# A batched matmul with transposed operands: both casts first, and the copies out of PSUM on two engines

## The chip, the cores and the metric

The kernel runs on one core of a Trainium2 chip. The metric is device time in microseconds (us) of one execution. The engines are named as in the profile: PE is TensorE (PEld its weight loads), DVE is VectorE, ACT is ScalarE, POOL is GpSimd, SP is SyncE, which here only issues DMAs.

## The reference

```python
batch, m, k, n = 16, 512, 512, 512
a: (batch, m, k) float32, b: (batch, n, k) float32
np.matmul(a, b.transpose(0, 2, 1)).astype(np.float32)
```

For each of the 16 batches it is a times b transposed. Both operands have the contracted index k last, while TensorE wants it on the partitions, so both have to be transposed on the way. In all 33.55 MB are read and 16.78 MB written.

## The kernel before

The work goes batch by batch, and the program order is written out by hand: each engine runs its instructions in the order in which the loop at the end of the kernel gives them.

For a batch, `load` (L46, L47) issues two DMAs from SP, 1 MB each, that bring a and b as tiles of 128 partitions x 2048 f32 (`a_sb`, `b_sb`; partition p has rows 4p to 4p+3). Five batches are loaded ahead (`AHEAD = 5`, six buffers for each operand); the load of batch i + 5 is issued after the store of batch i.

`turn` makes an operand ready. VectorE casts the whole tile to bf16 (`half`, L53). TensorE transposes it in 16 pieces of 128x128 (L59), eight into each of two PSUM tiles `tp`. VectorE copies each `tp`, 128 x 1024 bf16, into the SBUF tile `turned` (L64). There are four `tp` buffers, as many as a batch uses, and two of each `half` and `turned`. `turn` is called for a and then for b, so VectorE's program for a batch is: cast a, two copies of a, cast b, two copies of b.

`multiply` runs 16 matmuls of 128x512 (L72), four for each of four PSUM tiles `ps`. The first two of the four contract the part of k that is in the first `tp` of each operand, the third and fourth the part in the second. ScalarE copies each `ps` to `o_sb` (L77), and one DMA from SP stores the 1 MB of the batch (L84). There are five buffers of `o_sb`.

So TensorE's program for a batch is: 16 transposes of a, 16 transposes of b, 16 matmuls.

Of the kernel before, what the change touches and what calls it, by code (L numbers as in the profile page):

```python
# [1 line left out]

# [5 lines left out]


@with_exitstack  # L10
def kernel(
    ctx: ExitStack,
    tc: tile.TileContext,
    a: bass.AP,
    b: bass.AP,
    out: bass.AP,
):
    nc = tc.nc
    P = 128
    batch, M, K = a.shape  # L20
    _, N, _ = b.shape
    J = M // P
    KO = K // P
    f32 = mybir.dt.float32
    bf16 = mybir.dt.bfloat16
    AHEAD = 5

    const = ctx.enter_context(tc.tile_pool(name="ident", bufs=1))
    ident = const.tile([P, P], bf16)
    make_identity(nc, ident)  # L30

    apool = ctx.enter_context(tc.tile_pool(name="a_pool", bufs=6))
    bpool = ctx.enter_context(tc.tile_pool(name="b_pool", bufs=6))
    hpool = ctx.enter_context(tc.tile_pool(name="h_pool", bufs=2))
    tpool = ctx.enter_context(tc.tile_pool(name="t_pool", bufs=2))
    opool = ctx.enter_context(tc.tile_pool(name="o_pool", bufs=5))
    tppool = ctx.enter_context(tc.tile_pool(name="tp_pool", bufs=4, space=bass.MemoryType.PSUM))
    ppool = ctx.enter_context(tc.tile_pool(name="p_pool", bufs=4, space=bass.MemoryType.PSUM))

    def load(i):
        a_sb = apool.tile([P, J, K], f32, tag="a")
        b_sb = bpool.tile([P, J, K], f32, tag="b")
        nc.sync.dma_start(a_sb[:], a[i].rearrange("(p j) k -> p j k", j=J))  # L46
        nc.sync.dma_start(b_sb[:], b[i].rearrange("(p j) k -> p j k", j=J))  # L47
        return a_sb, b_sb

    def turn(src, tag):  # L50

        half = hpool.tile([P, J, K], bf16, tag="h" + tag)
        nc.vector.tensor_copy(out=half[:], in_=src[:])  # L53
        turned = tpool.tile([P, KO, J * P], bf16, tag="t" + tag)
        for ko in range(0, KO, 2):
            tp = tppool.tile([P, 2, J * P], bf16, tag="tp")
            for h in range(2):
                for j in range(J):
                    nc.tensor.transpose(  # L59
                        tp[:, h, j * P:(j + 1) * P],  # L60
                        half[:, j, (ko + h) * P:(ko + h + 1) * P],
                        ident[:],
                    )
            nc.vector.tensor_copy(out=turned[:, ko:ko + 2, :], in_=tp[:])  # L64
        return turned

    def multiply(aT, bT):
        o_sb = opool.tile([P, J, N], f32, tag="o")
        for j in range(J):
            ps = ppool.tile([P, N], f32, tag="p")  # L70
            for ko in range(KO):
                nc.tensor.matmul(  # L72
                    ps[:], aT[:, ko, j * P:(j + 1) * P], bT[:, ko, :],
                    start=(ko == 0), stop=(ko == KO - 1),
                )

            nc.scalar.copy(  # L77
                out=o_sb[:, j, :].rearrange("m (p j) -> m p j", j=J),
                in_=ps[:].rearrange("m (j p) -> m p j", j=J),
            )  # L80
        return o_sb

    def store(i, o_sb):
        nc.sync.dma_start(out[i].rearrange("(p j) n -> p j n", j=J), o_sb[:])  # L84

    loaded = {}
    with tc.manual_schedule():
        for i in range(min(AHEAD, batch)):
            loaded[i] = load(i)
        for i in range(batch):  # L90
            a_sb, b_sb = loaded.pop(i)
            aT = turn(a_sb, "a")
            bT = turn(b_sb, "b")
            o_sb = multiply(aT, bT)
            store(i, o_sb)
            if i + AHEAD < batch:
                loaded[i + AHEAD] = load(i + AHEAD)


# [1 line left out]
_INS = ['a', 'b']  # L101
_OUTS = [((16, 512, 512), 'float32')]


# [23 lines left out]
```

## Time and profile before

| | |
|---|---|
| median of 3 runs | 161.11 us (160.25 to 161.69) |
| the profiled execution | 161.58 us |
| its span, first to last instruction | 159.8 us |
| mean granted TensorE clock | 0.893 |
| busy: PE / DVE / ACT | 107.9 / 77.8 / 38.8 us |
| HBM read and written | 33.55 and 16.78 MB |

In the profile each row of a group names the line, the engine, the operation and the tiles it writes and reads, with buffer numbers left out. In a timeline, a row gives the start and the length of a run of like instructions, and in brackets the idle time of that engine ahead of it with what ended it. A wait row gives who waited for whom: the total, how many times, the longest. The "chain" is the sequence of work followed back from the last instruction, at each step to what released it. A row of a stretch gives the busy time of each engine in it, then the granted TensorE clock, the busy share of the 16 DMA engines, and the GB/s that they moved.

### The profile page before, as it was taken

Reading aid. Unit: us, or ns where it says so; the run is one execution under the profiler, and the core shown is the slowest. Engines: PE = TensorE matmul, PEld = TensorE weight load, DVE = VectorE, ACT = ScalarE, POOL = GpSimd, SP = SyncE. Lnnn points to the kernel's source line nnn. Section 1 sums busy time; section 2 is a strip of 40 time slices with the busy share of each in tenths; the row PEclk is TensorE's granted clock in tenths of the full one; section 3 lists DMA queues with packets and bytes.
Section 4 is the critical chain, followed back from the end, with each engine's and each line's share of the span. In section 5 each row is a group of like instructions: output and inputs, shape, how many; then the busy total and the mean of one; then the engine's idle time right before and its main releaser. Section 6 shows DMA issues by size and latency. Waiting matters only on the chain.

```text
span 159.8 us, 1885 instructions
## 1 busy us (share of the span) xinstructions
PE 107.9 (68%) x754; PEld 59.1 (37%) x768; DVE 77.8 (49%) x96; ACT 38.8 (24%) x65; POOL 0.7 (0%) x6
## 2 busy tenths in 40 slices
PE   0259767693958589494949769484867939394960
PEld 0243434343334345333434434344334525333420
DVE  0365383808456561826666380756547083836300
ACT  3001414050222305032321404141140505022140
POOL 1000000000000000000000000000000000000000
PEclk9999999789599968969995986999597799969789
DMA  4999999999999999997999799799974060603206
GB/s 164 427 427 429 425 425 369 429 408 427 412 431 425 420 427 420 386 410 299 367 416 322 310 320 431 248 375 398 357 304 170 2 263 0 263 4 164 98 0 263
DMA packets 6921, 50.46 MB, mean 316 GB/s; under 512 B 768, under 2 KB 768, under 8 KB 768
## 3 DMA queue, kind: packets, MB, share of 16 engines
q1 hardware_dynamic: 6912, 50.33, 78.6%
q8 instruction: 6, 0.10, 0.2%
q14 instruction: 3, 0.02, 0.0%
HBM read 33.55 MB, written 16.78 MB: 315 GB/s over the span
## 4 chain that ended last, share of the span: by engine, by line
PE 59%; DVE 31%; issue 3%; DMA 3%; ACT 1%; DVEq 0%; ACTq 0%
PE ps L72 46%; DVE turned L64 19%; PE tp L59 13%; DVE half L53 12%; DMA a_sb<-in_a_dram 3%; ACT o_sb L77 1%; DVEq L64 0%; ACTq L77 0%
## 5 line engine op out<-in xcount | busy, mean ns | idle before, releaser
L72 PE MATMUL ps<-turned 128*128 128x512 bf16 x242 | 74.6, 461 | 6.7 <-DVE turned L64 5.5
L64 DVE COPY turned<-tp 128x1024 bf16<-128x1024 bf16 x64 | 41.4, 686 | 66.4 <-PE tp L59 66.4
L77 ACT COPY o_sb<-ps 128x512 f32<-128x512 f32 x64 | 37.5, 586 | 115.5 <-PE ps L72 104.1
L59 PE MATMUL tp<-ident,half 128*128 128x128 bf16 x512 | 35.6, 225 | 39.8 <-DVE half L53 39.8
L59 PEld LDWEIGHTS <-half 128*128 128x128 bf16 x512 | 31.3, 101 | 46.1 <-DVE half L53 42.6
L72 PEld LDWEIGHTS <-turned 128*128 128x128 bf16 x256 | 27.8, 114 | 48.7 <-issue 25.6
L53 DVE CAST half<-a_sb 128x2048 bf16<-128x2048 f32 x16 | 19.5, 1218 | 5.5 <-DMA a_sb<-in_a_dram 5.5
L53 DVE CAST half<-b_sb 128x2048 bf16<-128x2048 f32 x16 | 19.5, 1216 | 0.0
L77 ACT ACT_TABLE_LOAD x1 | 1.3, 1283 | 0.7 <-PEq L112 0.7
masks.py:199 POOL TENSOR_SCALAR_AFFINE_SELECT ident<-ident 128x128 bf16<-128x128 bf16 x1 | 0.3, 294 | 0.1
masks.py:197 POOL MEMSET ident<- 128x128 bf16 x1 | 0.2, 205 | 0.3 <-POOLq L112 0.3
L112 POOL MEMSET const-bfloat16-1.0<- 128x1 bf16 x1 | 0.1, 102 | 0.0
L112 POOL MEMSET const-uint8-127<- 128x1 uint8 x1 | 0.1, 102 | 0.0
L112 POOL MEMSET const-float32-0.0<- 128x1 f32 x1 | 0.1, 99 | 0.2 <-issue 0.2
L112 POOL MEMSET const-float32-1.0<- 128x1 f32 x1 | 0.1, 99 | 0.0
## 6 DMA issues: line engine op xcount, KB each, us to landing
a_sb<-in_a_dram SPq DMA_DIRECT2D x16, 1024.0 KB, 9.1
b_sb<-in_b_dram SPq DMA_DIRECT2D x16, 1024.0 KB, 11.1
out_dram<-o_sb SPq DMA_DIRECT2D x16, 1024.0 KB, 4.9
```

Source lines behind the costliest of these rows:

```text
L53: nc.vector.tensor_copy(out=half[:], in_=src[:])
L59: nc.tensor.transpose(tp[:, h, j * P:(j + 1) * P], half[:, j, (ko + h) * P:(ko + h + 1) * P], ident[:],)
L64: nc.vector.tensor_copy(out=turned[:, ko:ko + 2, :], in_=tp[:])
L72: nc.tensor.matmul(ps[:], aT[:, ko, j * P:(j + 1) * P], bT[:, ko, :], start=(ko == 0), stop=(ko == KO - 1),)
L77: nc.scalar.copy(out=o_sb[:, j, :].rearrange("m (p j) -> m p j", j=J), in_=ps[:].rearrange("m (j p) -> m p j", j=J),)
L112: nc = _bacc.Bacc("TRN2", target_bir_lowering=False, num_devices=1)
```

## The change

The cast is taken out of `turn` into a function of its own, `halve`, and both operands of a batch are cast before either is transposed. `turn` is given the function that copies `tp` to `turned`: ScalarE's copy for a, VectorE's for b, as it was.

```diff
-    def turn(src, tag):
-
+    def halve(src, tag):
         half = hpool.tile([P, J, K], bf16, tag="h" + tag)
         nc.vector.tensor_copy(out=half[:], in_=src[:])
+        return half
+
+    def turn(half, tag, copy):
+
         turned = tpool.tile([P, KO, J * P], bf16, tag="t" + tag)
...
-            nc.vector.tensor_copy(out=turned[:, ko:ko + 2, :], in_=tp[:])
+            copy(out=turned[:, ko:ko + 2, :], in_=tp[:])
...
-            aT = turn(a_sb, "a")
-            bT = turn(b_sb, "b")
+            a_h = halve(a_sb, "a")
+            b_h = halve(b_sb, "b")
+            aT = turn(a_h, "a", nc.scalar.copy)
+            bT = turn(b_h, "b", nc.vector.tensor_copy)
```

With the lines that it adds, the cast is L52 in the changed kernel, the transposes L62, the copies of `tp` L67, the matmuls L75, the output copies L80 and the store L87.

On VectorE, the program begins so before (the first batch, and the cast that begins the second):

```order
L123 UNCONDITIONAL_BRANCH
L53 CAST half<-a_sb 128x2048
L64 COPY turned<-tp 128x1024 x2
L53 CAST half<-b_sb 128x2048
L64 COPY turned<-tp 128x1024 x2
L53 CAST half<-a_sb 128x2048
```

and so with the change, up to the second batch's copies of b:

```order
L128 UNCONDITIONAL_BRANCH
L52 CAST half<-a_sb 128x2048
L52 CAST half<-b_sb 128x2048
L67 COPY turned<-tp 128x1024 x2
L52 CAST half<-a_sb 128x2048
L52 CAST half<-b_sb 128x2048
L67 COPY turned<-tp 128x1024 x2
```

The two copies of a are gone from VectorE, and the two casts of a batch stand together, directly behind the copies of b of the batch before.

On ScalarE there was nothing but the 64 output copies; with the change its program begins so:

```order
L128 UNCONDITIONAL_BRANCH
L67 ACT_TABLE_LOAD
L67 COPY turned<-tp 128x1024 x2
L80 COPY o_sb<-ps 128x512 x4
L67 COPY turned<-tp 128x1024 x2
L80 COPY o_sb<-ps 128x512 x4
```

Two copies of a stand ahead of the four output copies of each batch, and so behind the four of the batch before. The programs of TensorE, SP and GpSimd hold the same operations in the same order as before.

## The prediction

> **What bounds the kernel now.** I read the shares of the engines first, then the chain that ended last, then the waits, then one batch in the timeline, and the DMA rows last.
>
> ```profile
> PE 107.9 (68%) x754; PEld 59.1 (37%) x768; DVE 77.8 (49%) x96; ACT 38.8 (24%) x65; POOL 0.7 (0%) x6
> ...
> PE 59%; DVE 31%; issue 3%; DMA 3%; ACT 1%; DVEq 0%; ACTq 0%
> PE ps L72 46%; DVE turned L64 19%; PE tp L59 13%; DVE half L53 12%; DMA a_sb<-in_a_dram 3%; ACT o_sb L77 1%; DVEq L64 0%; ACTq L77 0%
> ```
>
> No engine is full. The chain of the last-ended work goes back and forth between TensorE (59%) and VectorE (31%), and ScalarE has only 1% of it while it is busy for 24% of the span. So VectorE is in the way although it is busy only half of the time. The table of waits says where:
>
> ```profile
> PE tp L59 <- DVE half L53: 39.8, 17, 6.8
> DVE half L53 <- DMA a_sb<-in_a_dram: 5.5, 1, 5.5
> ```
>
> TensorE's transposes wait 39.8 us in 17 waits for casts, while the casts wait for data once, at the start. One batch in the timeline shows the loop:
>
> ```profile
> 45.07 1.06 PE L59 MATMUL tp<-ident,half 128*128 128x128 bf16 x16
> ...
> 45.27 0.59 ACT L77 COPY o_sb<-ps 128x512 f32<-128x512 f32 x1 [0.28 <-PE ps L72]
> 45.72 1.29 DVE L64 COPY turned<-tp 128x1024 bf16<-128x1024 bf16 x2 [4.13 <-PE tp L59]
> ...
> 46.92 1.22 DVE L53 CAST half<-b_sb 128x2048 bf16<-128x2048 f32 x1
> ...
> 48.20 1.07 PE L59 MATMUL tp<-ident,half 128*128 128x128 bf16 x16 [2.07 <-DVE half L53]
> 48.85 1.29 DVE L64 COPY turned<-tp 128x1024 bf16<-128x1024 bf16 x2 [0.71 <-PE tp L59]
> ...
> 49.60 3.77 PE L72 MATMUL ps<-turned 128*128 128x512 bf16 x15 [0.34 <-DVE turned L64]
> 50.06 1.22 DVE L53 CAST half<-a_sb 128x2048 bf16<-128x2048 f32 x1
> ...
> 53.21 1.00 PE L59 MATMUL tp<-ident,half 128*128 128x128 bf16 x15
> ```
>
> VectorE sits 4.13 us idle, copies a out at 45.72, and only then casts b (46.92 to 48.14), although b has long been there; TensorE stands still for 2.07 us until 48.20. Cast a is different: it runs at 50.06 beside the matmuls and costs nothing. From the transposes of a to the matmuls are 4.53 us (45.07 to 49.60), the matmul phase is 3.61 us (49.60 to 53.21), the cycle 8.14. Not every cycle is that short:
>
> ```profile
> 17.80 1.06 PE L59 MATMUL tp<-ident,half 128*128 128x128 bf16 x16
> ...
> 62.67 1.06 PE L59 MATMUL tp<-ident,half 128*128 128x128 bf16 x16
> ...
> 67.20 5.33 PE L72 MATMUL ps<-turned 128*128 128x512 bf16 x15 [0.34 <-DVE turned L64]
> 72.37 1.06 PE L59 MATMUL tp<-ident,half 128*128 128x128 bf16 x16
> ...
> 144.58 1.06 PE L59 MATMUL tp<-ident,half 128*128 128x128 bf16 x16
> ```
> ```profile
> 68.00:70.00 2.00, 2.00 (x6) 0.70 (x5) 0.87 (x1) 0.59 (x1) 0.00 (x0) 0.50 1.06 418
> ```
>
> The cycle from 62.67 to 72.37 takes 9.70: the same 4.53 ahead of the matmuls, then 5.17 for them, with a granted clock (the column ahead of the last two) of 0.50 in part of it. Between 17.80 and 144.58 lie 14 cycles, 9.06 us on the average, so the mean matmul phase is 4.53.
>
> The DMA engines come next, since they limit what a faster loop can bring. The rows are stretches with DMA share and GB/s at the end; below them are the times from issue to landing of the stores issued at 18.62 and at 63.48.
>
> ```profile
> DMA  4999999999999999997999799799974060603206
> ```
> ```profile
> 0.00:2.00 2.00, 0.00 (x0) 0.00 (x0) 0.00 (x0) 1.26 (x1) 0.70 (x6) 1.00 0.11 16
> ...
> 18.00:66.00 48.00, 33.13 (x255) 18.68 (x258) 26.65 (x33) 12.31 (x21) 0.00 (x0) 0.89 1.01 418
> 156.00:158.00 2.00, 0.00 (x0) 0.00 (x0) 0.00 (x0) 0.00 (x0) 0.00 (x0) 1.00 1.01 418
> 158.00:160.00 2.00, 0.00 (x0) 0.00 (x0) 0.00 (x0) 0.00 (x0) 0.00 (x0) 0.93 0.16 66
> ```
> ```profile
> out_dram<-o_sb SPq DMA_DIRECT2D x1, 1024.0 KB, 13.1
> ```
> ```profile
> out_dram<-o_sb SPq DMA_DIRECT2D x1, 1024.0 KB, 5.3
> ```
>
> The engines are full at 418 GB/s up to 66 us, but with a stock: 10 MB of loads are issued ahead of time, and the backlog melts (a store lands 13.1 us after its issue, later 5.3). After it is gone the DMA row shows gaps and, from slice 31, mostly nothing. The kernel is bound by the cycle of 9.06 us; the transfers of a batch (3 MB, 3 x 1.049 MB / 418 GB/s = 7.53 us) lie only a little beneath it. That is the next wall.
>
> **The change, part by part.** Durations:
>
> ```profile
> L64 DVE COPY turned<-tp 128x1024 bf16<-128x1024 bf16 x64 | 41.4, 686 | 66.4 <-PE tp L59 66.4
> L77 ACT COPY o_sb<-ps 128x512 f32<-128x512 f32 x64 | 37.5, 586 | 115.5 <-PE ps L72 104.1 <-remote 11.4
> ...
> L53 DVE CAST half<-a_sb 128x2048 bf16<-128x2048 f32 x16 | 19.5, 1218 | 5.5 <-DMA a_sb<-in_a_dram 5.5
> L53 DVE CAST half<-b_sb 128x2048 bf16<-128x2048 f32 x16 | 19.5, 1216 | 0.0
> ```
>
> *The cast of b moves ahead.* On VectorE both casts (1.22 + 1.22 = 2.44 us) now stand before the copies of b, which in the steady loop puts them behind the previous batch's copies, beside its matmuls. TensorE no longer waits between its two groups of transposes.
>
> *Two copies a batch go to ScalarE.* The trace has no ScalarE copy of 128x1024 bf16. Nearest row: 128x512 f32 at 0.586. If bytes count (both read 2 KB a partition), it is 0.586; if elements count and nothing is fixed, 1.172. I take 1.05, near the upper end, since the row is of another type but the same kind of copy, and a part of it may be fixed. ScalarE goes to 4 x 0.586 + 2 x 1.05 = 4.4 us a batch, still free for a quarter of the new cycle. [...]
>
> Now the new cycle, with 0 at the start of the transposes of a. From 45.07 and 45.72, eight transposes are ready after 0.65; the groups of 15 and 16 above (1.00 and 1.06) differ by 0.06, and 16 in 1.06 with the first 8 at 0.65 make some 0.43 for eight more. So the halves are ready at 0.65, 1.06, 1.5 and 1.93. ScalarE has the last output copy of the batch before until 0.79 (45.27 + 0.59 less 45.07), which is what stands ahead of the new copies in its queue; a is copied from 0.80 to 1.85 and to 2.90. VectorE copies b from 1.5, done at 2.2 and, two taking 1.29, at 2.8. The matmuls start 0.75 after the copy began (48.85 to 49.60), at 2.25, and their third needs both second copies: it waited for VectorE's before (that is inside the 3.61), and waits 0.1 more for ScalarE's now. Cycle: 2.25 + 3.61 + 0.1 = 5.96; with 1.172 a copy, 0.3 more; with 0.586, 0.1 less. VectorE's casts for the next batch end at 2.8 + 2.44 = 5.24, ahead of 5.96, so the matmuls hide them with 0.7 to spare. The gain in the loop is 4.53 - 2.35 = 2.18 us a batch.
>
> *Queues.* TensorE's, SP's and POOL's programs keep their order, so no transfer is issued in another place. On VectorE a cast that waits for data has behind it only the other cast and b's copies of the same batch, which need it anyway. On ScalarE a's copies now stand behind the output copies of the batch before, which wait for matmuls already ahead in TensorE's queue, and, from the sixth batch on, for the store of five batches ago; that store stands in SP's queue ahead of the loads of this same batch, so it is never late for it.
>
> *The first batch.* b's load, issued at 1.17, lands after 6.8:
>
> ```profile
> 1.17 0.42 SPq L47 DMA_DIRECT2D b_sb<-in_b_dram  x1
> ```
> ```profile
> b_sb<-in_b_dram SPq DMA_DIRECT2D x1, 1024.0 KB, 6.8
> ```
> ```profile
> 10.60 1.89 PE L59 MATMUL tp<-ident,half 128*128 128x128 bf16 x16 [1.92 <-DVE half L53]
> 12.42 5.54 PE L72 MATMUL ps<-turned 128*128 128x512 bf16 x16
> ```
>
> Landed at 7.97, cast by 9.2, transposed and copied in the 1.82 of before (10.60 to 12.42), so matmuls from 11.05 instead of 12.42. Batch 1 starts at about 17.0 at the latest (17.80 now; the slow clock of the start may eat a part).
>
> *What is late next.* Without data to wait for, the last matmul would end near 17.0 + 15 x 5.96 = 106.4, and the end come some 5.5 later, at 112. The data can't follow: a batch is 7.53 us of transfers. After some eight batches the backlog of loads is used up, the casts wait for DMA, and the queue stays full to the end. So the span is that of the transfers: 50.46 MB (the page's total) at 418 GB/s = 120.7; 2.0 before it starts (first row of stretches); 158 + 0.3 = 158.3 is when the last bytes move and 159.8 the end, so 1.5 behind. Sum 124.2.
>
> *The tail.* Behind the last pair of loads, SP's queue has four stores (batches 11 to 14) and the last. Four are 10.0 us; in that time batch 15 must be cast and multiplied.
>
> ```profile
> 149.11 5.34 PE L72 MATMUL ps<-turned 128*128 128x512 bf16 x15 [0.34 <-DVE turned L64]
> ```
> ```profile
> 155.10 0.33 SPq L84 DMA_DIRECT2D out_dram<-o_sb  x1
> ```
> ```profile
> out_dram<-o_sb SPq DMA_DIRECT2D x1, 1024.0 KB, 3.8
> ```
>
> The store at 155.10 lands at 158.9, 0.6 after its last bytes, and took 0.7 to begin (3.8 - 2.5 - 0.6). So: landing 0.6, cast 1.22, 1.40 to the matmuls (48.20 to 49.60), 6.0 to the issue at the slow clock (149.11 to 155.10), 0.7: 9.9 against 10.0. It just fits; I add 0.3 for what may miss. That makes a span of 124.5 and, with the 1.78 that the profiled execution has around it (161.58 less 159.8), a time of 126.3. The median of 161.11 is 0.3% below that execution, which I leave out.
>
> **The rivals.**
>
> 1. *The clock eats it.* If every matmul phase were at the slow 5.17, the cycle would be 2.35 + 5.17 = 7.52, level with the transfers; batches then end at 17.0 + 15 x 7.52 + 5.5 = 135.3, so 137 in time. With the mean phase of 4.53 it is 6.88 and 125.7 from the loop alone, so 127.5 in time; halfway between the two is 132, which I take as this rival's price. For it: waits for data lengthen TensorE's pauses again. Against it: where a pause is for data, the transfers set the time anyway, and the pause in the loop falls from 4.53 to 2.35. [...]
>
> 2. *ScalarE's copy is slow, and the kernel slower than before.* If a copy takes x, the third matmul starts at 0.85 + 2x and the cycle is 3.86 + 2x; the matmul pause is then as long as now, so the phase is up to 1.56 longer: 5.42 + 2x. That passes today's 9.06 from x = 1.82. I price it a little past that point, at three times VectorE's row of 0.686: x = 2.06, cycle 9.54, and with a first batch 1 us later 18 + 15 x 9.54 + 5.5 = 166.6, time 168. Against it: 0.586 for half the elements; 1.82 would be three times that row. [...]
>
> 3. *The transfers are slower, or faster, than 418* when ScalarE, VectorE and stores crowd together:
>
> ```profile
> 36.00:40.00 4.00, 1.59 (x25) 1.25 (x23) 3.26 (x5) 0.17 (x1) 0.00 (x0) 1.00 1.03 428
> 26.00:30.00 4.00, 1.93 (x33) 1.73 (x31) 2.69 (x4) 0.59 (x1) 0.00 (x0) 1.00 0.99 373
> ```
>
> At 428: 117.9 + 3.8 = 121.7, time 123.5. At 373, around the first store: 135.3 + 3.8 = 139.1, time 141. The 48 us mean, with its share of stores in it, speaks for 418.
>
> 4. *Nothing happens*, because the transfers already set the time up to 66 us. Against it: the melting backlog, and casts that wait for data only once. Time 161.
>
> **How the numbers follow.** Forecast 0.74; clock 0.12; slower transfers 0.07; slow copy 0.05; nothing 0.02. The range goes from the faster transfers, 123.5, to the price of the clock rival, 132, which holds a little over 8 in 10. Faster by over 1% (what a measurement of this kernel can tell) holds the forecast, the clock and the transfers: 0.93; within 1%: 0.02; slower: 0.05.
>
> **What would show it.** The DMA row full to about slice 39; VectorE's casts waiting mainly for DMA, with TensorE's wait for casts inheriting that; ScalarE's copies near 1.05 and ScalarE busy some 72 us (38.8 + 32 x 1.05); VectorE some 56 (77.8 - 32 x 0.686); transposes of b right behind those of a. Wrong it is if ScalarE's copy is well over 1.2, if the DMA row has gaps with casts waiting for nothing, or if the rate in the full stretches is not 418.

## The result, and the profile after

The changed kernel takes 126.79 us (median of 4 runs, 126.48 to 126.86) against 161.4 of the kernel before (median of 4, 160.25 to 161.99): a ratio of 0.7859, with a 95% interval of 0.7811 to 0.7906. The forecast was 126.3, with 123.5 to 132. The profiled execution has a span of 124.9 us; 124.5 was forecast. An execution that took over 1.5% longer than the fastest of its kernel is left out of the times and ratios below.

The page of the changed kernel, with the lines that answer to those shown of before:

```profile
PE 92.2 (74%) x754; PEld 55.9 (45%) x768; DVE 59.2 (47%) x64; ACT 68.3 (55%) x97; POOL 0.7 (1%) x6
...
PEclk9999999999999999999999999999999999999995
DMA  3999999999999999999999999999999999999982
...
DMA 80%; DVE 6%; PE 5%; SPq 3%; issue 1%; ACT 0%; DVEq 0%
DMA b_sb<-in_b_dram 80%; DVE half L52 4%; PE ps L75 3%; PE tp L62 2%; DVE turned L67 2%; SPq L46 1%; SPq L47 1%; ACT o_sb L80 0%; DVEq L52 0%
```

The DMA row has no gap left, and the chain that was TensorE and VectorE is now 80% a load. The clock row, too, is full up to the last slice, in which no work is left. In the table of waits the casts now wait for data, and TensorE waits for the casts behind them:

```profile
DVE half L52 <- DMA a_sb<-in_a_dram: 22.0, 11, 5.6
PE tp L62 <- DVE half L52: 20.0, 12, 6.9
...
DVE half L52 <- DMA b_sb<-in_b_dram: 14.8, 12, 1.3
```

The timeline has two kinds of batches. While loads lie in stock, a batch looks like this:

```profile
27.29 1.95 PE L62 MATMUL tp<-ident,half 128*128 128x128 bf16 x32
27.49 0.59 ACT L80 COPY o_sb<-ps 128x512 f32<-128x512 f32 x1 [0.28 <-PE ps L75]
27.99 1.93 ACT L67 COPY turned<-tp 128x1024 bf16<-128x1024 bf16 x2
...
28.83 1.29 DVE L67 COPY turned<-tp 128x1024 bf16<-128x1024 bf16 x2 [2.34 <-PE tp L62]
...
29.57 3.78 PE L75 MATMUL ps<-turned 128*128 128x512 bf16 x15 [0.34 <-DVE turned L67]
...
30.04 1.22 DVE L52 CAST half<-a_sb 128x2048 bf16<-128x2048 f32 x1
...
31.17 1.22 DVE L52 CAST half<-b_sb 128x2048 bf16<-128x2048 f32 x1
...
33.19 1.95 PE L62 MATMUL tp<-ident,half 128*128 128x128 bf16 x32
```

All 32 transposes run in one piece, the matmuls start 2.28 us after the first of them, both casts lie beside the matmuls, and the cycle is 5.90 us. Later a batch looks like this:

```profile
87.43 1.23 DVE L52 CAST half<-a_sb 128x2048 bf16<-128x2048 f32 x1 [1.68 <-DMA a_sb<-in_a_dram]
...
88.82 1.06 PE L62 MATMUL tp<-ident,half 128*128 128x128 bf16 x16
...
89.88 1.23 DVE L52 CAST half<-b_sb 128x2048 bf16<-128x2048 f32 x1 [1.23 <-DMA b_sb<-in_b_dram]
...
91.17 1.07 PE L62 MATMUL tp<-ident,half 128*128 128x128 bf16 x16 [1.29 <-DVE half L52]
...
92.58 3.78 PE L75 MATMUL ps<-turned 128*128 128x512 bf16 x15 [0.34 <-DVE turned L67]
...
96.19 1.06 PE L62 MATMUL tp<-ident,half 128*128 128x128 bf16 x16
```

Each cast waits for its own load, and the cycle is 7.37 us. Three stretches of the transfers (granted clock, DMA share and GB/s at the end) show the steady rate and the two places that fall below it:

```profile
24.00:29.00 5.00, 4.94 (x46) 3.16 (x46) 2.66 (x4) 3.29 (x7) 0.00 (x0) 1.00 1.01 354
60.00:110.00 50.00, 38.11 (x318) 22.66 (x322) 25.45 (x28) 28.30 (x41) 0.00 (x0) 1.00 1.01 425
118.00:120.00 2.00, 0.46 (x3) 0.00 (x0) 0.00 (x0) 0.80 (x2) 0.00 (x0) 1.00 0.73 307
```

### The profile page after: what moved, and what is told of

Read it like the earlier page. It is cut to its first block, busy times and chain, and to the rows that moved or that the text cites. A ratio compares the mean times of both kernels' runs of the same rounds, so it can differ in the third digit from the quotient of the medians.

```text
span 124.9 us, 1885 instructions
## 1 busy us (share of the span) xinstructions
PE 92.2 (74%) x754; PEld 55.9 (45%) x768; DVE 59.2 (47%) x64; ACT 68.3 (55%) x97; POOL 0.7 (1%) x6
## 4 chain that ended last, share of the span: by engine, by line
DMA 80%; DVE 6%; PE 5%; SPq 3%; issue 1%; ACT 0%; DVEq 0%
DMA b_sb<-in_b_dram 80%; DVE half L52 4%; PE ps L75 3%; PE tp L62 2%; DVE turned L67 2%; SPq L46 1%; SPq L47 1%; ACT o_sb L80 0%; DVEq L52 0%
## 5 line engine op out<-in xcount | busy, mean ns | idle before, releaser
L75 PE MATMUL ps<-turned 128*128 128x512 bf16 x242 | 59.8, 382 | 6.1 <-DVE turned L67 5.5
L80 ACT COPY o_sb<-ps 128x512 f32<-128x512 f32 x64 | 37.5, 586 | 44.0 <-PE ps L75 40.8
L62 PE MATMUL tp<-ident,half 128*128 128x128 bf16 x512 | 34.8, 225 | 20.1 <-DVE half L52 20.0
L62 PEld LDWEIGHTS <-half 128*128 128x128 bf16 x512 | 31.3, 101 | 25.6 <-DVE half L52 23.7
L75 PEld LDWEIGHTS <-turned 128*128 128x128 bf16 x256 | 25.1, 98 | 36.6 <-issue 10.7
L67 ACT COPY turned<-tp 128x1024 bf16<-128x1024 bf16 x32 | 30.8, 1016 | 6.0 <-PE tp L62 6.0
L52 DVE CAST half<-a_sb 128x2048 bf16<-128x2048 f32 x16 | 19.6, 1224 | 22.0 <-DMA a_sb<-in_a_dram 22.0
L67 DVE COPY turned<-tp 128x1024 bf16<-128x1024 bf16 x32 | 20.7, 686 | 19.3 <-PE tp L62 19.3
L52 DVE CAST half<-b_sb 128x2048 bf16<-128x2048 f32 x16 | 19.6, 1226 | 14.8 <-DMA b_sb<-in_b_dram 14.8
## 6 DMA issues: line engine op xcount, KB each, us to landing
a_sb<-in_a_dram SPq DMA_DIRECT2D x16, 1024.0 KB, 19.6
b_sb<-in_b_dram SPq DMA_DIRECT2D x16, 1024.0 KB, 19.6
out_dram<-o_sb SPq DMA_DIRECT2D x16, 1024.0 KB, 19.6
```

Source lines behind the costliest of these rows:

```text
L62: nc.tensor.transpose(tp[:, h, j * P:(j + 1) * P], half[:, j, (ko + h) * P:(ko + h + 1) * P], ident[:],)
L75: nc.tensor.matmul(ps[:], aT[:, ko, j * P:(j + 1) * P], bT[:, ko, :], start=(ko == 0), stop=(ko == KO - 1),)
L80: nc.scalar.copy(out=o_sb[:, j, :].rearrange("m (p j) -> m p j", j=J), in_=ps[:].rearrange("m (j p) -> m p j", j=J),)
```

## The experiments

The theory: the cast of b waited behind the copies of a on VectorE; with it moved, the loop falls below the time of a batch's transfers, and these set the time. Rivals: the copies on ScalarE are what helps; the length of the loop still counts; something other than the transfers holds the cycle at 7.37 us.

### Casts first, without ScalarE

```diff
-            aT = turn(a_h, "a", nc.scalar.copy)
+            aT = turn(a_h, "a", nc.vector.tensor_copy)
```

> Both casts first, but VectorE copies a and b; ScalarE has its output copies alone. Theory (the transfers set the time, at 7.37 us a batch in the changed kernel, and the loop has only to be shorter): VectorE copies a until 1.94 us after the transposes begin and b until 3.2, so the third matmul starts at 3.23 instead of 2.85 and the loop takes 6.3 us instead of 5.9, still under 7.37: 126.8 us, between 126 and 128. Rival (the loop's length counts in the time): 15 x 0.38 us more, 132.5. Rival (the gain came from the copies on ScalarE): about 160.

Measured: 126.73 us, ratio to the kernel before 0.7873 (0.7839 to 0.7908). The changed kernel, run again beside it, had:

> The changed kernel as it is, on the same chip as its variants: 126.5 to 127.0 us by every theory.

It took 126.69, ratio 0.7875 (0.7845 to 0.7906). The two can't be told apart. The timeline shows the loop with data in stock, at 6.21 us, and the same 80% of a load in its chain:

```profile
27.21 1.95 PE L62 MATMUL tp<-ident,half 128*128 128x128 bf16 x32
...
33.42 1.95 PE L62 MATMUL tp<-ident,half 128*128 128x128 bf16 x32
```
```profile
DMA 80%; issue 4%; DVE 4%; PE 3%; SPq 3%; ACT 0%; DVEq 0%
```

So the order of the casts alone brings the whole gain. The other part alone was not run: with a's copies on ScalarE, VectorE's program is cast a, cast b, copies of b, whichever of the two source orders is written, and the programs of all engines come out the same as the changed kernel's. So each part is enough by itself, since each takes the copies of a out from between the casts.

### The other half of the copies on ScalarE

VectorE casts a, copies a, casts b, as before; ScalarE copies b.

```diff
-            b_h = halve(b_sb, "b")
-            aT = turn(a_h, "a", nc.scalar.copy)
-            bT = turn(b_h, "b", nc.vector.tensor_copy)
+            aT = turn(a_h, "a", nc.vector.tensor_copy)
+            b_h = halve(b_sb, "b")
+            bT = turn(b_h, "b", nc.scalar.copy)
```

> Half of the copies on ScalarE as in the change, but those of b: VectorE casts a, copies a, casts b, and ScalarE copies b. Theory (what counts is that the cast of b stands ahead of the wait for a's transposes): cast b ends at 3.1 us as before, b's copies at 1.02 each end at 4.8 and 5.8, the loop is 5.85 + 3.0 = 8.9 us at the full clock, and the pause between matmul phases is longer than before, so the clock falls at least as often: 160 to 172 us, mean clock 0.9 or lower. Rival (taking half of the copies off VectorE is what counts): 127 to 135.

Measured: 177.08 us (176.03 to 177.92), ratio 1.0995 (1.0931 to 1.106); slower than before, though it has the same share of copies on ScalarE as the change.

```profile
48.66 1.06 PE L62 MATMUL tp<-ident,half 128*128 128x128 bf16 x16
...
49.30 1.29 DVE L67 COPY turned<-tp 128x1024 bf16<-128x1024 bf16 x2 [6.68 <-PE tp L62]
...
50.51 1.22 DVE L52 CAST half<-b_sb 128x2048 bf16<-128x2048 f32 x1
...
51.78 1.07 PE L62 MATMUL tp<-ident,half 128*128 128x128 bf16 x16 [2.07 <-DVE half L52]
52.50 1.93 ACT L67 COPY turned<-tp 128x1024 bf16<-128x1024 bf16 x2 [3.05 <-PE tp L62]
...
53.56 0.68 PE L75 MATMUL ps<-turned 128*128 128x512 bf16 x2 [0.71 <-ACT turned L67]
```

The wait of 2.07 us for the cast of b is back to the hundredth, and ScalarE's slower copy is now on the path: 4.90 us from the transposes to the matmuls (4.53 before). Its mean cycle in the profile (an execution of 178.79 us with a mean clock of 0.855; the three others have 0.853 to 0.862), from the second batch's transposes at 18.00 to the last batch's at 161.30, is 10.24 us, so 5.34 for the matmul phase, and every one of the 14 is that long: each has a stretch of the slow clock (a mean of 0.855 leaves 51 of the 177.0 us at half the clock, 3.4 for each of the 15 phases after the first). I had expected 172 at most: the direction held, but I had counted on some phases at the full clock, and there are none.

### Fewer transfers

To see the loops without the wall, b is loaded for batch 0 only, and every batch casts that tile again; this leaves out 15 of the 48 transfers, and the products are with the first b.

```diff
-        nc.sync.dma_start(b_sb[:], b[i].rearrange("(p j) k -> p j k", j=J))
-        return a_sb, b_sb
+        if i == 0:
+            b_one.append(bpool.tile([P, J, K], f32, tag="b", name="b_sb"))
+            nc.sync.dma_start(b_one[0][:], b[i].rearrange("(p j) k -> p j k", j=J))
+        return a_sb, b_one[0]
```

The kernel before, so treated:

> The kernel before with less to load: b of batch 0 alone is loaded, and every batch casts and uses that tile (so a third of the transfers is left out, and the products are with the first b). Theory (the loop set the time before, the transfers did not): the loop stays at 8.14 us or 9.7 with the slow clock, 158 to 163 us. Rival (transfers were part of the time before, through the full first 66 us): 145 or less.

The casts first, all copies on VectorE:

> Both casts first, all copies of tp on VectorE, with b of batch 0 alone loaded and used for every batch. Theory (without the wall of transfers the loop shows): 6.3 us a batch, 110 + 15 x 0.38 = 115.5 us in span, 117.5 in time, 116 to 119. Rival (this order of VectorE is as good as the change in the loop itself too): 111 to 113. Rival (something else than the transfers holds the loop at 7.37): 126.

The changed kernel:

> The changed kernel with b of batch 0 alone loaded and used for every batch. Theory (without the wall of transfers the loop shows): 5.9 us a batch as between 27.3 and 39.1 us in the changed kernel's timeline; the second batch starts at 15.5, the last at 98.1, the end comes some 12 later: span 110, time 112, 110 to 114. Rival (something else than the transfers holds the loop at 7.37): 126.

| b loaded once | time, us | with all loads |
|---|---|---|
| kernel before | 161.64 | 161.4 |
| casts first | 115.23 | 126.73 |
| the change | 112.26 | 126.79 |

Nearly a third of the transfers less does nothing for the kernel before (1.0031, 0.9993 to 1.0069): it was bound by its loop although its DMA row was full for the first 66 us with all loads. The two others fall to their loops; the casts first come out below the 116 to 119 that I had expected. The transposes of the last two batches, casts first and then the change:

```profile
95.40 1.95 PE L63 MATMUL tp<-ident,half 128*128 128x128 bf16 x32
...
101.60 1.95 PE L63 MATMUL tp<-ident,half 128*128 128x128 bf16 x32
```
```profile
93.10 1.95 PE L63 MATMUL tp<-ident,half 128*128 128x128 bf16 x32
...
99.00 1.95 PE L63 MATMUL tp<-ident,half 128*128 128x128 bf16 x32
```

6.20 and 5.90 us a batch. Here the copies on ScalarE are worth 0.30 us a batch, and behind the wall nothing. The times differ by only 3.0 us (one run against the median of two), because the first matmul phase took 3.62 us in the profile of the casts first and 5.19 in that of the change. Of the 49.4 us that the change takes off the loop (161.64 less 112.26), the real kernel keeps 34.6; the transfers hide the other 14.8.

### The clock

Before, two matmul phases in three ran partly at half the clock (ten stretches of 3.41 us at 0.50); now, behind the first batch, none does (1.00 up to 122.16 us). To see whether that is a part of the gain, the kernel before got 24 more transposes of a behind its own, into a PSUM tile that nobody reads, in the time in which TensorE waits for the cast of b; `ps` has three buffers instead of four to make room.

```diff
+        if tag == "a":
+            for r in range(24):
+                nc.tensor.transpose(
+                    spare[:, 0, (r % J) * P:(r % J + 1) * P], half[:, r % J, 0:P], ident[:],
+                )
         return turned
```

> The kernel before, with 24 more transposes of a's cast tile behind those of a, into a spare PSUM tile that nobody reads (three buffers of ps instead of four make room). They fill 1.3 of the 2.07 us in which TensorE waits for the cast of b and are over before it; the chain stays as it was. [...] Rival (only the matmuls count, and their pause of 4.53 us stays): 159 to 163 us and clock 0.89.

And with three buffers alone:

> The kernel before with three buffers of ps instead of four and nothing else: 160 to 162 us by every theory, since each ps is copied out 0.9 us after it is complete and the fourth buffer is not waited for.

If work of any kind in the gap keeps the clock up, every cycle is 8.14 us, and I had put the time at 145 to 149. Measured: 145.44 us against 160.67 of the kernel before beside it, ratio 0.903 (0.8975 to 0.9085), with a mean clock of 0.991; three buffers alone 160.93 (1.0009, 0.9978 to 1.004), clock 0.891.

```profile
49.19 1.06 PE L59 MATMUL tp<-ident,half 128*128 128x128 bf16 x16
...
50.08 1.50 PE L67 MATMUL spare<-ident,half 128*128 128x128 bf16 x24
...
52.32 1.07 PE L59 MATMUL tp<-ident,half 128*128 128x128 bf16 x16 [0.73 <-DVE half L53]
...
53.72 1.62 PE L77 MATMUL ps<-turned 128*128 128x512 bf16 x6 [0.34 <-DVE turned L64]
```

The transposes of b still start 3.13 us after those of a, and the matmuls 4.53 after; only the clock is another, and the cycle is 8.15 us (122.50 to 130.65). So the useless work saves 15.2 us. TensorE's stall cost twice: its own 2.07 us a batch, and on the average 0.92 of slow matmuls behind it (4.53 less 3.61). So of the 3.16 us by which the change shortens the cycle while data lie in stock (9.06 less 5.90), 0.92 come from the clock.

### The last store

At 118 to 120 us the DMA engines run short (a share of 0.73, 307 GB/s), waiting for the last batch. Its store was cut into four, each behind its own output copy:

```diff
+        if i < batch - 1:
+            nc.sync.dma_start(view, o_sb[:])
+        else:
+            for j in range(J):
+                nc.sync.dma_start(view[:, j, :], o_sb[:, j, :])
```

> The changed kernel, with the last batch's store issued as four of 256 KB, each behind its own output copy. Theory (the transfers run out of work while the last batch is finished: 369 and 246 GB/s in the two stretches from 118 to 120 us): three quarters of the last store start up to 2.6 us earlier, the hole of some 0.6 us closes and less is left behind the last copy: 125.0 to 126.2 us. Rival (the end is a fixed latency, or short transfers cost what the hole gave): 126.8 or more.

Measured: 127.06 us, no better than the 126.69 of the changed kernel beside it. The issue-to-landing times of the last store of the changed kernel, issued just before 119.4, and of the last quarter here:

```profile
out_dram<-o_sb SPq DMA_DIRECT2D x1, 1024.0 KB, 5.0
```
```profile
out_dram<-o_sb SPq DMA_DIRECT2D x1, 256.0 KB, 5.1
```

The hole did close (410 GB/s from 119 to 120 us, where the changed kernel has 246), but a quarter of the bytes landed no sooner after its issue than the whole, so the end stayed. What the hole gave was lost behind it: in the two microseconds from 121 on, the cut store moved at 258 and 137 GB/s, the whole one at 418 and 221. The cut store also went in packets of 2 KB, a row of one quarter, instead of 8 KB (1328 packets are under 8 KB and 816 of them under 2 KB; in the changed kernel all 769 under 8 KB are under 2 KB); whether that is the reason is open.

## Why the prediction was right

*The bound before.* The loop, and in it the cast of b behind the copies of a: shown by casts first (the wait gone, the whole gain there) and by the copies of b on ScalarE (the wait kept, no gain). That the loop and not the transfers set the time is shown by the loads left out.

*The new cycle.* 5.96 forecast, 5.90 measured; the matmuls start at 2.28 us, where 2.25 was put. ScalarE's copy, the one cost that no row of before had, was put at 1.05 and is 1.016:

```profile
L67 ACT COPY turned<-tp 128x1024 bf16<-128x1024 bf16 x32 | 30.8, 1016 | 6.0 <-PE tp L62 6.0
```

That is 1.73 times the 0.586 of the output copies, for twice their elements; by an estimate from these two rows, if the type makes no difference, 0.43 us of a copy goes with each 512 elements, and some 0.16 is fixed. The 0.1 for the wait on ScalarE's second copy was not needed: two copies in a row take 1.93 us and end 2.63 after the first transpose, not 2.90. The rival of a slow copy did not come about: 1.016 is 1.5 times VectorE's 0.686, and it needed 1.82. No run shows the factor of three at which it was priced, and ScalarE, busy for 55% of the span, had time to spare.

*What is late next.* The transfers, as forecast: they and what stands around them made 124.2 of the 124.5 of the span. Two terms were off and offset each other: the steady rate is 425 GB/s, not 418, and the rate falls to 354 around the first stores and to 307 in the tail, where I gave 0.3 us. The mean of 418 had a dip like the first in it (373 from 26 to 30 us); that what was left came out even is luck.

*When the data run short.* I put it after some eight batches; casts already wait in the sixth and seventh, since the loop starts earlier (15.48 for the second batch, not 17.0) and b of the sixth batch lands at 38.3 (issued at 17.16, 21.1 later) instead of the 35.2 that 13 transfers of 2.51 behind a start at 2.0, with 0.6 to land, would give. It changes nothing in the end, where only the sum of the transfers counts.

*The clock.* It was a rival, at a chance of 0.12, and it went the other way: 0.989 instead of 0.893. The prediction's sum did not rest on it, since the transfers took that place; but the phase of 3.61 in the cycle did, and it held in all 15 batches after the first. The reason given for it was not the right one. The prediction went by the pause between the matmuls, 4.53 us against 2.35. The pause of 4.53 was not idle: it has 2.13 us of transposes, and no stretch in it without work is longer than 2.07. With the spare transposes it stays at 4.53, and the clock at 0.991; in the changed kernel it is 3.8 once the data run short, at the full clock. What went with the change is the 2.07 us without work. Nor does the prediction's gain of 2.18 us a batch have the 0.92 of the clock in it, although its cycle of 5.96 does.

*What the prediction did not see.* It costed the two parts of the change together. That either alone would reach the wall was to be had from its own numbers: with all copies on VectorE the third matmul starts at 3.2 us instead of 2.9, and a loop of 6.3 is still shorter than 7.53.

## What to carry to other kernels

In an engine's program that is written out by hand, an instruction whose data are ready should not stand behind one that waits for another engine: here the order of two casts was worth 34 us of 161, and moving work to a free engine nothing on top of it. Before costing a faster loop, work out the next wall (here the bytes of a batch over the measured rate); here 14.8 of 49.4 us were hidden behind it, and one of two parts was enough. And a DMA row that is full for a while is no proof of a bound by transfers: look whether the time from issue to landing shrinks, as it did here while a stock of loads was used up. It fell from 13.1 to 5.3 us for the stores before; with the change it stays at 19.6, which is eight transfers of 2.46 us.

## What the runs showed of the hardware

In these runs TensorE's stall was paid for a second time by its clock, and transposes put into the stall were enough to keep the clock up. In the changed kernel the matmuls pause for 3.8 us of a cycle of 7.37 (from 88.8 to 92.58), with 32 transposes in the pause, and the clock stays at full speed (0.986 to 0.993 over four runs; in the profile what is missing lies behind the last matmul); in the kernel before the pause of 4.53 has the same 32 transposes, but 2.07 us without any work (1.29 in the changed kernel), and the clock falls in two cycles of three. Filling that gap with transposes alone, with the pause of the matmuls as it was, brought it from 0.89 to 0.991.

How much work stood ahead of the slow clock can be read from the trace of the kernel before. Its loop has ten stretches at a granted clock of 0.50, each 3.41 us long, and they start whole multiples of 3.41 us apart: the first four at 30.02, 40.26, 57.32 and 67.56 us, which is 3, 5 and 3 of them. In the 3.41 us ahead of each of the ten, TensorE is busy for 1.34 to 1.45 us, transposes counted (1.35 from 26.60 to 30.02). Cut into stretches of 3.41 us from 16.36 us to the last matmul, that trace has 1.50 us or more in every other one at the full clock. In the changed kernel, cut in the same way from 12.93 to 118.75 us, none has less than 1.77, and none is slow. With the spare transposes, the 3.41 us from 49.56 have transposes alone, 2.67 us of them, and the six matmuls behind them take 1.62 us; three took 1.46 at the slow clock before (from 30.48). (The ends of matmuls are modelled in the profile, so these are sums by its rows.) A rule for the clock these traces do not show.
